# Weight sums of the down projection two pairs later, last token tiles built in place, key sums among the norms, and 66 low halves on GpSimd

## The chip, the cores and the metric

The kernel runs on one core of a Trainium2 chip. The metric is the device time of one execution in microseconds, and the kernel of before stands at the median of three runs. Besides TensorE, VectorE, ScalarE and GpSimd, the text speaks of SyncE (SP), which issues nearly all DMA transfers. The profile names the engines PE, DVE, ACT, POOL and SP.

## What is computed

One step of a two-layer encoder for two groups of rows: 1024 prompt positions and 8 × 16 sample positions, 1152 rows of width 1024, in the kernel nine token tiles of 128 rows (tile 8 holds the samples). Each layer is an attention and a GEGLU feed-forward with a causal convolution, both modulated by `c` and closed by a layer norm:

```python
def conv_ffn(h, prev, w_up, conv_w, conv_b, w_down):
    u = h @ w_up
    ...
    ue = jnp.concatenate([prev.astype(u.dtype), u], axis=1)
    y = conv_b
    for tap in range(CONV_W):
        y = y + conv_w[tap] * ue[:, tap:tap + T]
    a, g = jnp.split(y, 2, axis=-1)
    out = (jax.nn.gelu(g) * a) @ w_down
    return out, ue[:, T:]
...
        x = layer_norm(DEEPNORM_ALPHA * x + (1 + g_m) * mix, ln_g[l, 0], ln_b[l, 0])
        h = x * (1 + sc_f) + sh_f
        f, conv_rows = conv_ffn(h, None if prompt else state_conv[l], w_up[l], conv_w[l], conv_b[l], w_down[l])
        x = layer_norm(DEEPNORM_ALPHA * x + (1 + g_f) * f, ln_g[l, 1], ln_b[l, 1])
        if l == N_A_LAYERS - 1:
            ada_kv = (sc @ w_ada_kv + b_ada_kv)[:, None, :]
            sh_kv, sc_kv = jnp.split(ada_kv, 2, axis=-1)
            kv = ((x * (1 + sc_kv) + sh_kv) @ w_kv_b).reshape(B, T, 2, N_HEADS_B, HEAD_DIM)
```

D_MODEL is 1024, D_FF 2816 and there are two layers. After layer 0 one pair of keys and values is projected from its output (`w_kv_b`) and used by the attention of layer 1.

## The kernel before

**Stages.** Opening, attention, output projection, feed-forward (`ffn`, L1331 and around it) and down projection (`down`, L1419 on) of layer 0; then keys and values (`kv`, L836 on), attention, output projection, feed-forward and down projection of layer 1. One scheduler lays the instructions of each engine in a row ahead of time, and every engine and every DMA queue runs its row in that order.

**Split numbers.** Every fp32 operand of a large product is cast to a high half on ScalarE (L177), and the rest is made by a subtraction, the low half (L188), on VectorE or GpSimd as the caller's letters say ("v" or "p"). A product is three passes of matmuls: low by high, high by low, high by high.

**Seven products.** The large products of the feed-forward, the keys and the down projection halve their blocks by Strassen's scheme in Winograd's form: of two by two blocks, seven products instead of eight, from sums of blocks. There are three kinds of sums:

- Token sums (`tsums`, L1124 to 1152). For each of the nine token tiles the modulated transpose is reloaded from DRAM (`hD`, L1131), four sums are made (L1135 to 1138) and three of them split. For the feed-forward L1135 and L1136 run on GpSimd and a fourth sum is collected and cast once at the end (H); for the keys all four run on VectorE and the fourth is split tile by tile.
- Sums of up-weights (`products`, L1177 to 1180, on GpSimd) for each of the column pairs j = 2 to 21 of the feed-forward (pairs 0 and 1 are multiplied plainly) and for the keys' four. The matmuls of a pair are L1229, its evictions L1190 (VectorE) and L1197 (ScalarE).
- Sums for the down projection, made in spare time during the pairs. Two 128 × 512 blocks of a gated row pair give activation sums (`act_sums`, GpSimd, L1343 to 1346). Two rows of `w_down` give a weight sum (`weight_sums`, L1351 to 1359): two loads (L1354), three operations on GpSimd (L1355 to 1357) and two stores (L1358, L1359). There are eleven of each in a layer, and the list `wsum` says in which pair each weight sum is issued: `[2, 3, 4, 6, 8, ..., 20]`.

**Down projection.** Its products come in the order q = 1, 2, 5, 6, 3, 7, 4, each with eleven steps of twelve matmuls (L1476), fifteen where samples join. A step fetches one activation block and one weight block (`fetch`, L1491), splits both, and multiplies. The activations lie in a ring of seven slots (`acts`); their low halves are made by VectorE (L1471). The two sums q5 and u4, which become the left and the right half of the output of tiles 4 to 7, and c11 and p1, for tiles 0 to 3, stay in SBUF. `head` (L1533) adds the residual row to the two halves of a tile, into the residual's buffer (its home), and starts the norm; `tail` (L1566) finishes it: transposes on TensorE (L1042), the affine step on ScalarE (L1054), split of the transposed rows for the key and value products (L188, GpSimd in layer 0), stores of `hD` and `hmD`, and the norm's weight and bias (L1065 on GpSimd, L1066 on VectorE). Tile 8 is finished in product 3, tiles 0 to 3 in product 7, and tiles 4 to 7 after product 4. In layer 0 `zt` and `hf` are buffers of a tail: the copy of the transposed rows (one buffer or two), and the modulated ones (`hfr`, two buffers).

**Keys and values.** The value tiles of the first half are multiplied (L319) between the tails of tiles 4 to 7 and after them. The token sums of the keys go through a ring of four reload buffers (`raws`), which lie where q5 and u4 end; then come the key products and the value tiles of the second half.

Of the kernel before, what the change touches and what calls it, by code (L numbers as in the profile page):

```python
# [102 lines left out]
class Trunk:  # L103
# [732 lines left out]
    def kv(self, hv, vv):  # L836
# [11 lines left out]

        T1S = F[:, 6180:8484].rearrange("p (k t i) -> p k t i", k=4, i=64)
        p1s = [F[:, 8484:8804], F[:, 8804:9060]]  # L850
# [30 lines left out]
        order = (0, 1, 2, 3, 8, 4, 5, 6, 7)  # L881
        raws = Ring([F[:, o : o + 1024] for o in (2048, 3072, 4096, 5120)])
        for t in order[0:5]:
# [4 lines left out]
        last = self.wslots[2:4] + [(X2[:, o : o + 1024], X2[:, o + 1024 : o + 2048]) for o in (0, 2048)]  # L888
        hv, vv = Ring([F[:, o : o + 1024].bitcast(F32R) for o in (0, 1024)]), Ring([F[:, o : o + 512] for o in (11108, 11620)])
        for t in order[5:]:  # L890
# [29 lines left out]
        w = vload(1, last)  # L920
        hv = Ring(hl)
        self.ws = narrow
# [321 lines left out]
    def ffn(self, l, xsrc, xdst, affs):  # L1244
# [152 lines left out]
        self.pend = []  # L1397
        wsum = [2, 3] + list(range(4, NFF - 1, 2))
        for j in range(NPL):
# [19 lines left out]
    def down(self, l, xsrc, xdst, affs, act_sums):  # L1419
# [3 lines left out]
        def quad(x):  # L1423
            return [x[:, i * 512 : i * 512 + 512] for i in range(4)]

        X2 = self.x2p.tile([128, 4608], F32, name="x2f", tag="x2")
        q5, u4 = quad(F[:, 0:2048]), quad(F[:, 2048:4096])
        c11, p1 = quad(X2[:, 0:2048]), quad(X2[:, 2048:4096])
# [7 lines left out]
        homes = {8: fa, 0: fb, 1: self.w0[1], 2: fa, 3: fb, 4: X2[:, 0:1024], 5: X2[:, 2048:3072], 6: fa, 7: fb}  # L1436
        if l:
            homes[6], homes[7] = self.hf, self.gateS
        xs = {}
# [7 lines left out]
        late = Ring(raws)  # L1447
        diffs = Ring([F[:, o : o + 512] for o in range(2048, 6144, 512)])
        subs = self.subslots(ws[1:4])
# [13 lines left out]

        def act(src, sample=None):
            n = 512 if sample is None else 640
            hi, lo = (t[:, 0:n] for t in acts.next())
            raw = lo.bitcast(F32)
            nc.sync.dma_start(raw[:, 0:512], src)
            if sample is not None:
                nc.sync.dma_start(raw[:, 512:640], sample)  # L1470
            self.split(raw, hi, lo, "a", "v")  # L1471
            return hi, lo
# [18 lines left out]
        def fetch(q, m):  # L1491
# [15 lines left out]
            elif q == 6:  # L1507
                a, w = act(actS[m, 0][:, lo_half], sample(o)), weight(wT[m, 1][:, hi_half])
                w2 = weight(wdn[o][:, hi_half], late)
            elif q == 3:  # L1510
                a, w = act(actS[m, 1][:, lo_half]), weight(wdn[o][:, hi_half], late)
            elif q == 7:
                a, w = act(actS[m, 0][:, hi_half]), weight(wT[m, 0][:, hi_half])
            else:
                a, w = act(prompt(o, hi_half)), weight(wT[m, 1][:, lo_half])
            return a, w, w2 or w
# [17 lines left out]
        def head(t):  # L1534
# [5 lines left out]
            else:  # L1540
                parts = [q5[t - 4], u4[t - 4]]
            x = row = xs.pop(t)
            sm = self.sm.next() if l else None
            heads[t] = row, sm
# [58 lines left out]
        def tails(k):  # L1603
            def hook(m):
                if m in TAILS[k]:
                    t = TAILS[k][m]
                    tail(t)
                    rows(*{0: (3,), 1: (4, 5), 2: (6,), 3: (7,)}.get(t, ()))

            return hook  # L1610
# [29 lines left out]
        if not l:  # L1640
            self.take_w0(F32R)
            ev = [X2[:, o : o + 1024].bitcast(F32R) for o in (1024, 3072)], [X2[:, 4096:4608]]
            self.kvrun = self.kv(*ev)
# [292 lines left out]
```

## Time and profile before

| what | us |
| --- | --- |
| runs | 2814.4, 2820.66, 2827.81 |
| median | 2820.66 |
| profiled execution | 2813.54 |
| its span, from first to last instruction | 2811.8 |
| token sums of the feed-forward, layer 0 and layer 1 | about 485 to 541, 2020 to 2072 |
| pairs 2 to 21, layer 0 and layer 1 | 541 to 1050, 2072 to 2540 |
| down projection, layer 0 and layer 1 | 1050 to 1320, 2540 to 2812 |
| of it in layer 0, product 3 from, 7 from, 4 from | 1215, 1248, 1281 |
| keys and values, first half | 1320 to 1400 |

A row of the timeline has the start in the span, the duration, the engine, the line and operation, output and inputs by the program's names, the shape, and how many instructions in a row it stands for; in brackets stands how long the engine was idle before it, and which engine, buffer and line ended that. A group's row has the count, the busy time, the mean in ns and the idle time before. All positions are those of the profiled execution.

### The profile page before, as it was taken

The numbers are of one execution on the slowest core, as the hardware profiler recorded it, in microseconds if no ns is written. First come the engines' busy times: TensorE is split into PE (matmuls) and PEld (weight loads), VectorE is DVE, ScalarE is ACT, GpSimd is POOL, SyncE is SP. The second block draws the span as 40 slices with busy tenths as digits, with TensorE's granted clock in tenths as the row PEclk, the third lists the DMA queues.
The fourth block names the chain that finished last, engine by engine and source line by source line (L and its number), as shares of the span: only waits on it lengthen the run. The fifth ranks groups of instructions, "written<-read, shape, count | busy, mean of one in ns | idle before, by whom it ended". The sixth has DMA issues, their size and how long they took to land.

```text
span 2811.8 us, 47453 instructions
## 1 busy us (share of the span) xinstructions
PE 2657.6 (95%) x17134; PEld 2341.9 (83%) x17134; DVE 2031.0 (72%) x4010; ACT 1393.4 (50%) x2912; POOL 1031.4 (37%) x808
## 2 busy tenths in 40 slices
PE   7999889989999999998899999989989999999997
PEld 5887768889999997877798888867889999997775
DVE  4376767777777785679654677767888888885668
ACT  3475724443444344455636666663444444444554
POOL 2132523456555642112420122242465656542101
PEclk9999999999999999999999999999999999999998
DMA  8756444575565557675767467764453433347664
GB/s 296 222 163 190 141 131 158 186 275 198 190 206 201 186 169 245 199 246 194 279 205 266 114 162 197 215 193 142 156 189 112 143 134 130 132 145 249 199 211 151
DMA packets 252715, 528.59 MB, mean 188 GB/s; under 512 B 40032, under 2 KB 100400, under 8 KB 252480
## 3 DMA queue, kind: packets, MB, share of 16 engines
q1 hardware_dynamic: 252480, 525.56, 56.9%
q8 instruction: 135, 2.21, 0.3%
q14 instruction: 100, 0.82, 0.1%
HBM read 391.12 MB, written 143.77 MB: 190 GB/s over the span
## 4 chain that ended last, share of the span: by engine, by line
PE 69%; DVE 11%; DMA 10%; POOL 4%; issue 3%; ACT 3%; SPq 1%; DVEq 0%; POOLq 0%; ACTq 0%
PE PS L1229 26%; PE PS L1476 15%; PE PS L319 10%; PE PS L306 7%; PE PS L602 2%; PE PS L580 2%; DVE wl L188 2%; PE PS L234 2%; PE PS L551 1%; DMA w0f<-in_wdn_dram 1%; PE PS L293 1%; DMA actS<-F 1%; DMA ws<-in_adaw_dram 1%; DVE F L518 1%; PE PS L554 1%
## 5 line engine op out<-in xcount | busy, mean ns | idle before, releaser
L1229 PE MATMUL PS<-H,wh 128*128 128x256 f32 (+1 forms) x2624 | 408.6, 298 | 0.0
L1476 PE MATMUL PS<-wh,xa 128*128 128x512 f32 x1144 | 366.5, 400 | 17.5 <-ACT wh L177 6.4
L1229 PEld LDWEIGHTS PS<-H,wh 128*128 128x128 f32 x2624 | 373.1, 192 | 0.4 <-issue 0.4
L188 DVE TENSOR_TENSOR wl<-F,wh 128x512 fp32r<-128x512 f32 (+2 forms) x278 | 274.2, 996 | 31.6 <-ACT wh L177 29.1
L1190 DVE TENSOR_TENSOR F<-PS,F 128x320 f32<-128x320 f32 (+1 forms) x446 | 196.4, 450 | 130.3 <-PE PS L1229 129.2
L1476 PEld LDWEIGHTS PS<-wh,xa 128*128 128x128 f32 x1144 | 216.9, 190 | 74.4 <-ACT wh L177 12.4
L177 ACT CAST wh<-F 128x512 fp32r<-128x512 f32 (+2 forms) x278 | 163.7, 598 | 219.4 <-PE PS L1229 132.5
L1229 PE MATMUL PS<-H,wl 128*128 128x256 f32 (+1 forms) x1312 | 234.3, 301 | 22.2 <-ACT F L1197 15.8
L1476 PE MATMUL PS<-wl,xa 128*128 128x512 f32 x572 | 228.1, 400 | 0.4 <-DVE wl L188 0.4
L1229 PEld LDWEIGHTS PS<-H,wl 128*128 128x128 f32 x1312 | 196.7, 193 | 30.8 <-ACT F L1197 16.2
L1321 ACT ACTIVATE PS<-F 128x512 f32<-128x512 f32 x160 | 124.6, 779 | 187.6 <-DVE F L1323 107.2
L188 DVE TENSOR_TENSOR xa<-xa 128x640 fp32r<-128x640 f32 (+1 forms) x154 | 128.0, 836 | 122.2 <-ACT xa L177 121.1
L1229 PE MATMUL PS<-xa,wh 128*128 128x320 f32 (+1 forms) x1328 | 203.8, 296 | 0.0
L1331 POOL TENSOR_TENSOR F<-F 128x1152 f32<-128x1152 f32 x44 | 125.6, 2855 | 188.9 <-DVE F L1323 147.7
L177 ACT CAST xa<-xa 128x640 fp32r<-128x640 f32 (+1 forms) x154 | 104.0, 682 | 178.2 <-DMA xa<-actD 118.2
L1229 PEld LDWEIGHTS PS<-xa,wh 128*128 128x128 f32 x1328 | 186.3, 189 | 0.0
L177 ACT CAST wh<-ws 128x512 fp32r<-128x512 f32 (+1 forms) x153 | 104.3, 691 | 97.8 <-PE PS L1229 30.2
L1065 POOL TENSOR_TENSOR F<-F 128x1024 f32<-128x1024 f32 x24 | 58.6, 2443 | 227.8 <-PE PS L1042 95.1
L188 DVE TENSOR_TENSOR wl<-ws,wh 128x512 fp32r<-128x512 f32 (+1 forms) x135 | 135.7, 1011 | 8.4 <-ACT wh L177 7.9
L640 POOL TENSOR_TENSOR F<-F,x2r 64x512 f32<-64x512 f32 x62 | 79.4, 1281 | 168.2 <-DVE F L616 147.2
L319 PE MATMUL PS<-xa,H 128*128 128x512 f32 x504 | 133.3, 405 | 6.2 <-ACT xa L177 3.3
L306 PE MATMUL PS<-H,w0r 128*128 128x384 f32 (+1 forms) x720 | 138.3, 342 | 0.0
(349 smaller groups left out, 6384.2 us busy)
## 6 DMA issues: line engine op xcount, KB each, us to landing
ws<-in_adaw_dram SPq DMA_DIRECT2D x64, 512.0 KB
ws<-in_wup_dram SPq DMA_DIRECT2D x49, 512.0 KB
F<-in_adaw_dram SPq DMA_DIRECT2D x48, 512.0 KB
w0f<-in_wdn_dram SPq DMA_DIRECT2D x44, 512.0 KB
actS<-F SPq DMA_DIRECT2D x44, 512.0 KB
xa<-actS SPq DMA_DIRECT2D x88, 256.0 KB
F<-in_wup_dram SPq DMA_DIRECT2D x39, 512.0 KB
xa<-actD SPq DMA_DIRECT2D x66, 256.0 KB
```

Of the source, the lines that this page charges most:

```text
L177: nc.scalar.copy(out, in_)
L188: self.eng(el).tensor_sub(lo, src, hi.bitcast(F32))
L234: mm = nc.tensor.matmul(ps[32 * j : 32 * j + 32, hf * 256 : hf * 256 + 256], self.cT[:, k * 32 : k * 32 + 32], w[:, j * 256 : j * 256 + 25 ...
L306: mm = self.nc.tensor.matmul(out[:, 0:n], w[a][:, k * 128 : k * 128 + 128], H[:, p, k, s0 : s0 + n], start=i == 0, stop=i == 23)
L319: self.nc.tensor.matmul(out[:, 0:n], H[:, p, j * kn + k, t0 : t0 + 128], w[a][:, k * n : k * n + n], start=i == 0, stop=i == 23,)
L640: self.eng("v" if last else "p").tensor_mul(on[r, q], on[r, q], rb[r, :])
L1065: self.eng(er[0]).tensor_mul(xr, x, self.lng)
L1190: nc.vector.tensor_add(d, v(ps), a if len(a.shape) == 3 else v(a))
L1229: self.pairmm = nc.tensor.matmul(ps[:, 0:m], w[a][:, k * 128 : k * 128 + 128], x(p, k, n), start=start and c == 0, stop=c == 11, skip_grou ...
L1321: nc.scalar.activation(ps, u[:, 2 + o : 514 + o], AF.Identity, **aff)
L1331: nc.gpsimd.tensor_mul(yg, yg, ya)
L1476: self.downmm = nc.tensor.matmul(ps, a[p][:, i * 128 : i * 128 + 128], w[q], start=first and c == 0, stop=last and c == 2, skip_group_chec ...
```

## The change

Four edits:

1. `wsum` becomes `[4, 5, 6, 7, 8, 10, ..., 20]`: the first weight sum is issued in pair 4, and pairs 4 to 8 have one each.
2. In `down`, q5 and u4 are interleaved, so that the two halves of a tile 4 to 7 are 1024 neighbouring columns, and `head` writes the sum of these tiles there, in place, instead of into the residual's home. The homes of tiles 6 and 7 in layer 0 move, and both residuals are loaded after tail 3. The ring of weight differences (`diffs`) uses the gaps. The last four tails of layer 0 get one `hf` buffer, and `zt` lies at `fa`.
3. In `kv`, the buffers of the value tiles move, and the reload ring of the key sums has three slots, at columns 0 to 3071, which come free tile by tile; T1S moves by 36 columns.
4. `act` takes an engine for the low half, and products 3, 7 and 4 name GpSimd: 33 subtractions of 128 × 512 in each layer.

```diff
@@ kv
-        T1S = F[:, 6180:8484].rearrange("p (k t i) -> p k t i", k=4, i=64)
+        T1S = F[:, 6144:8448].rearrange("p (k t i) -> p k t i", k=4, i=64)
...
-        raws = Ring([F[:, o : o + 1024] for o in (2048, 3072, 4096, 5120)])
+        raws = Ring([F[:, o : o + 1024] for o in (0, 1024, 2048)])
...
-        hv, vv = Ring([F[:, o : o + 1024].bitcast(F32R) for o in (0, 1024)]), Ring([F[:, o : o + 512] for o in (11108, 11620)])
+        hv = Ring([F[:, o : o + 1024].bitcast(F32R) for o in (8448, 3072)])
...
-        hv = Ring(hl)
+        hv, vv = Ring(hl), Ring([F[:, o : o + 512] for o in (11108, 11620)])
@@ ffn
-        wsum = [2, 3] + list(range(4, NFF - 1, 2))
+        wsum = list(range(4, 9)) + list(range(10, NFF - 1, 2))
@@ down
-        q5, u4 = quad(F[:, 0:2048]), quad(F[:, 2048:4096])
+        q5, u4 = ([F[:, i * 1024 + o : i * 1024 + o + 512] for i in range(4)] for o in (0, 512))
...
-        if l:
-            homes[6], homes[7] = self.hf, self.gateS
+        homes[6], homes[7] = (self.hf, self.gateS) if l else (X2[:, 1024:2048], X2[:, 3072:4096])
...
-        diffs = Ring([F[:, o : o + 512] for o in range(2048, 6144, 512)])
+        diffs = Ring([F[:, o : o + 512] for o in (2560, 3584, 4096, 4608, 5120, 5632, 1536, 512)])
...
-        def act(src, sample=None):
+        def act(src, sample=None, el="v"):
...
-            self.split(raw, hi, lo, "a", "v")
+            self.split(raw, hi, lo, "a", el)
...
             elif q == 3:
-                a, w = act(actS[m, 1][:, lo_half]), weight(wdn[o][:, hi_half], late)
+                a, w = act(actS[m, 1][:, lo_half], el="p"), weight(wdn[o][:, hi_half], late)
             elif q == 7:
-                a, w = act(actS[m, 0][:, hi_half]), weight(wT[m, 0][:, hi_half])
+                a, w = act(actS[m, 0][:, hi_half], el="p"), weight(wT[m, 0][:, hi_half])
             else:
-                a, w = act(prompt(o, hi_half)), weight(wT[m, 1][:, lo_half])
+                a, w = act(prompt(o, hi_half), el="p"), weight(wT[m, 1][:, lo_half])
...
             x = row = xs.pop(t)
+            if 4 <= t < 8:
+                row = F[:, (t - 4) * 1024 : (t - 4) * 1024 + 1024]
...
-                    rows(*{0: (3,), 1: (4, 5), 2: (6,), 3: (7,)}.get(t, ()))
+                    rows(*{0: (3,), 1: (4, 5), 3: (6, 7)}.get(t, ()))
...
             self.take_w0(F32R)
-            ev = [X2[:, o : o + 1024].bitcast(F32R) for o in (1024, 3072)], [X2[:, 4096:4608]]
+            rings = Ring([fa]), Ring([self.hf])
+            ev = [F[:, 8448:9472].bitcast(F32R)], [F[:, 9472:9984]]
```

In GpSimd's row, the token sums of a feed-forward (L1135, L1136) read like this before from the sixth tile on; L1355 to L1357 are the first weight sum, L1331 the gating product of pair 1, and L1407 clears edges of the first Strassen pair.

```order
L1135 TENSOR_TENSOR F<-F 128x4x64
L1136 TENSOR_TENSOR F<-F 128x4x64
L1355 TENSOR_TENSOR w0f<-w0f 128x512
L1331 TENSOR_TENSOR F<-F 128x1152
L1356 TENSOR_TENSOR w0f<-w0f 128x512
L1135 TENSOR_TENSOR F<-F 128x4x64 x3
L1357 TENSOR_TENSOR w0f<-w0f 128x512
L1136 TENSOR_TENSOR F<-F 128x4x64 x3
L1407 MEMSET F 128x2
```

The same four tiles in the changed kernel:

```order
L1135 TENSOR_TENSOR F<-F 128x4x64
L1287 TENSOR_TENSOR F<-F 128x8x2
L1136 TENSOR_TENSOR F<-F 128x4x64
L1331 TENSOR_TENSOR F<-F 128x1152
L1135 TENSOR_TENSOR F<-F 128x4x64 x2
L1136 TENSOR_TENSOR F<-F 128x4x64
L1135 TENSOR_TENSOR F<-F 128x4x64
L1136 TENSOR_TENSOR F<-F 128x4x64 x2
L1407 MEMSET F 128x2
```

The three operations of the weight sum are gone from between the token sums; layer 1 reads the same way.

In GpSimd's row in the down projection of layer 0, before, the weight differences (L1503) are followed by nothing but tails, each an L1065 (norm weight) and a split (L188 into H), from tile 8 on:

```order
L1503 TENSOR_TENSOR F<-F 128x512 x7
L1065 TENSOR_TENSOR F<-F 128x1024
L188 TENSOR_TENSOR H<-F,H 128x8x128
L1065 TENSOR_TENSOR F<-F 128x1024
L188 TENSOR_TENSOR H<-F,H 128x8x128
L1065 TENSOR_TENSOR w0f<-w0f,F 128x1024
```

In the changed kernel, from the same place to tile 2, the activations' low halves are the rows with xa (lines here are those of the changed file, in which `fetch` stands one line higher):

```order
L188 TENSOR_TENSOR xa<-xa 128x512 x8
L1065 TENSOR_TENSOR F<-F 128x1024
L188 TENSOR_TENSOR xa<-xa 128x512
L188 TENSOR_TENSOR H<-F,H 128x8x128
L188 TENSOR_TENSOR xa<-xa 128x512 x16
L1065 TENSOR_TENSOR F<-F 128x1024
L188 TENSOR_TENSOR xa<-xa 128x512
L188 TENSOR_TENSOR H<-F,H 128x8x128
L188 TENSOR_TENSOR xa<-xa 128x512
L1065 TENSOR_TENSOR w0f<-w0f,F 128x1024
L188 TENSOR_TENSOR xa<-xa 128x512
L188 TENSOR_TENSOR H<-F,H 128x8x128
```

Twenty-five low halves stand ahead of tile 0's split and seven or eight more among the tails of tiles 0 to 2.

In VectorE's row where the tails of tiles 4 to 7 end and the key sums begin (L1066 is a tail's norm bias, L866 a value tile's low half, L1135 to L1138 a token tile's sums), before:

```order
L1066 TENSOR_TENSOR x2f<-x2f,F 128x1024
L866 TENSOR_TENSOR x2f<-PS,x2f 128x8x64 x2
L1066 TENSOR_TENSOR F<-F 128x1024
L866 TENSOR_TENSOR F<-PS,F 128x8x64
L1066 TENSOR_TENSOR F<-F 128x1024
L866 TENSOR_TENSOR F<-PS,F 128x8x64
L1135 TENSOR_TENSOR F<-F 128x4x64 x3
L1136 TENSOR_TENSOR F<-F 128x4x64 x3
```

and in the changed kernel, from the same tile's L1066, that of tile 5:

```order
L1066 TENSOR_TENSOR F<-F 128x1024
L1135 TENSOR_TENSOR F<-F 128x4x64
L866 TENSOR_TENSOR F<-PS,F 128x8x64
L1136 TENSOR_TENSOR F<-F 128x4x64
L1137 TENSOR_TENSOR F<-F 128x4x64
L1138 TENSOR_TENSOR F<-F 128x4x64
L188 TENSOR_TENSOR xa<-F,xa 128x4x64 x2
L188 TENSOR_TENSOR x2r<-F,x2r 128x4x64
L1066 TENSOR_TENSOR F<-F 128x1024
L866 TENSOR_TENSOR F<-PS,F 128x8x64
L1135 TENSOR_TENSOR F<-F 128x4x64
L1136 TENSOR_TENSOR F<-F 128x4x64
```

The first tile's sums stand before the norm bias of tile 6, and two more tiles' before that of tile 7.

## The prediction

> **What bounds the kernel now.** I read the page first, then the chain of the run, then what TensorE waited for.
>
> ```profile
> span 2811.8 us, 47453 instructions
> PE 2657.6 (95%) x17134; PEld 2341.9 (83%) x17134; DVE 2031.0 (72%) x4010; ACT 1393.4 (50%) x2912; POOL 1031.4 (37%) x808
> ...
> PE 69%; DVE 11%; DMA 10%; POOL 4%; issue 3%; ACT 3%; SPq 1%; DVEq 0%; POOLq 0%; ACTq 0%
> ```
>
> TensorE is busy 95% of the span and 69% of the final chain is its own, so about 150 us of 2811.8 are idle, and only idle time that ends because of an edited step can be won. The list of TensorE's waits (line waiting, what ended the wait: total, times, longest) names these:
>
> ```profile
> PE PS L1229 <- ACT F L1197: 15.8, 2, 8.9
> ...
> PE PS L1229 <- ACT xa L177: 9.1, 2, 8.9
> ...
> PE PS L319 <- DVE F L1634: 4.4, 1, 4.4
> ```
>
> The 15.8 us are one stall at the first pair after the token sums in each FFN; the 9.1 hold one of 8.9 before the key products; the 4.4 stand where the last token tiles begin. Next, busy time by stage (start:end length, then PE, PEld, DVE, ACT, POOL busy with counts, granted clock, DMA share, GB/s): the layer-1 token sums, steady pairs, the down product 7, the product 4, the tails beside the value tiles, and the key sums.
>
> ```profile
> 2030.00:2072.00 42.00, 33.08 (x195) 32.88 (x193) 37.43 (x70) 22.62 (x49) 22.83 (x27) 0.94 0.56 188
> 600.00:700.00 100.00, 98.95 (x768) 91.06 (x767) 73.53 (x110) 37.56 (x71) 60.67 (x47) 0.99 0.58 198
> 1240.00:1280.00 40.00, 40.00 (x177) 32.32 (x176) 36.85 (x87) 23.89 (x41) 6.57 (x2) 1.00 0.70 240
> 1280.00:1320.00 40.00, 37.06 (x164) 29.45 (x163) 36.60 (x43) 23.34 (x50) 17.23 (x7) 0.96 0.66 229
> 1340.00:1370.00 30.00, 30.00 (x149) 24.82 (x148) 11.08 (x18) 24.89 (x55) 20.30 (x12) 1.00 0.86 329
> 1370.00:1406.00 36.00, 26.08 (x140) 23.11 (x140) 33.14 (x92) 20.51 (x60) 12.05 (x5) 0.86 0.69 246
> ```
>
> In the token sums VectorE is busy 37.43 of 42 us and TensorE idles: VectorE sets the end there. In steady pairs TensorE is busy 98.95 of 100, so GpSimd's 60.67 cost nothing. In 1340 to 1370 TensorE is full and VectorE does only 11.08; right behind it VectorE has 33.14 of 36 and TensorE stops. That unevenness is what the key part of the change touches.
>
> **Part 1: weight sums start two pairs later.** The timeline of the layer-1 token sums (start, duration, engine, line, operands, and in brackets the idle time before it and who ended it):
>
> ```profile
> 2047.83 1.47 POOL L1355 TENSOR_TENSOR w0f<-w0f 128x512 f32<-128x512 f32 x1
> 2048.07 1.51 DVE L1137 TENSOR_TENSOR F<-F 128x256 f32<-128x256 f32 x1
> ...
> 2050.52 4.15 DVE L188 TENSOR_TENSOR xa<-F,xa 128x256 fp32r<-128x256 f32 x2 [0.48 <-ACT xa L177]
> ...
> 2052.91 1.48 POOL L1356 TENSOR_TENSOR w0f<-w0f 128x512 f32<-128x512 f32 x1
> ...
> 2055.58 0.32 SPq L1131 DMA_DIRECT2D F<-hD  x1
> ...
> 2059.70 0.75 PE L1229 MATMUL PS<-H,wl 128*128 128x320 f32 x4
> ...
> 2060.28 1.34 PE L1229 MATMUL PS<-H,wh 128*128 128x320 f32 x8
> 2060.32 1.30 POOL L1357 TENSOR_TENSOR w0f<-w0f 128x512 f32<-128x512 f32 x1
> ...
> 2061.58 2.31 POOL L1136 TENSOR_TENSOR F<-F 128x256 f32<-128x256 f32 x3
> ...
> 2071.97 1.44 PE L1229 MATMUL PS<-H,wl 128*128 128x320 f32 x4 [8.92 <-ACT F L1197]
> ...
> 2073.20 2.33 PE L1229 MATMUL PS<-H,wh 128*128 128x320 f32 x8
> ```
>
> L1355 to L1357 are the first weight sum. While L1355 runs (2047.83 to 2049.30), L1137 on VectorE takes 1.51 where the same shape takes about 0.42 (L1135 in the key sums' rows below): 1.1 lost. The two splits at L188 take 4.15 instead of 0.83 across L1331 and L1356; L1331 stays, L1356 owns about 1.4 of that. L1357 stands straight ahead of the last three L1136, whose tiles end the stage: 1.3. All three lie in front of the stall that ends at 2071.97, so 1.1 + 1.4 + 1.3 = 3.8 comes off it, and in layer 0, where the same three sums stand in the same places, the same. The weight sum's two loads and two stores leave SyncE's row there as well; the last reload of a tile was issued at 2055.58 between them and lands earlier, which I count as nothing, since VectorE is full. The stall of layer 0, and a later one:
>
> ```profile
> 540.64 1.43 PE L1229 MATMUL PS<-H,wl 128*128 128x320 f32 x4 [6.87 <-ACT F L1197]
> ...
> 596.57 2.90 DVE L188 TENSOR_TENSOR wl<-ws,wh 128x512 fp32r<-128x512 f32 x2
> ...
> 597.83 1.43 PE L1229 MATMUL PS<-H,wl 128*128 128x320 f32 x4 [4.25 <-DVE wl L188]
> ```
>
> After a stall the first four matmuls take 1.43 to 1.44 and the next eight 2.33; ahead of it the same shapes take 0.75 and 1.34 (at 2059.70 and 2060.28), so each stall costs some 2 us more behind it. With 8.92 − 3.8 = 5.1 left in layer 1 I count 0.5 of that as saved, per layer. Sum for both layers: 2 × (3.8 + 0.5) = 8.6, say −9. By the Trainium skill (TensorE: Matmul & The Clock Gate, section "HAM oscillation — how this bites in real kernels") the clock drops only behind gaps longer than about 3.4 us; the rows agree, and by that rule layer 0, left with 6.87 − 3.8 = 3.1, would keep full clock and the sum would be about 2 lower; I don't use this.
>
> The row at 597.83 is the second gain: the up-weight of pair 3 is split only from 596.57 to 599.47, with the loads, stores and sums of pairs 2 and 3's weight sums on the same queue and on GpSimd. Its 4.25 and some 2 of slow clock make 6.3; with those transfers two pairs later I take −5, bounds −6.3 (all of it theirs) to 0 (other background loads fill the gap).
>
> The moved sums now come in five pairs in a row (4 to 8) instead of every second one. Each is three GpSimd ops, 1.47 + 1.48 + 1.30 = 4.3 us in the rows above, with two 512 KB loads and two stores. A pair is 168 matmuls, so 100 us with 768 hold 4.6 pairs of 22 us, and GpSimd is busy 13 in each (60.67 in all): 4.3 more fits. The skews of layer 0 (L1673) share the queue. I take +1, bounds 0 to +4, a second late up-weight like the one above. Part 1: −9 − 5 + 1 = **−13**; bounds −18 (both stalls lose their slow clock too) to −3 (the two gains of layer 0's pairs lost, +4).
>
> **Part 2: 66 low halves to GpSimd.** The prices, from the groups by form (count, busy, mean ns, idle before); VectorE from 1210 to 1320,
>
> ```profile
> L188 DVE TENSOR_TENSOR xa<-xa 128x512 fp32r<-128x512 f32 x30 | 22.8, 767 | 6.3 <-ACT xa L177 6.2
> ```
>
> and the same view of GpSimd over the whole run:
>
> ```profile
> L1065 POOL TENSOR_TENSOR F<-F 128x1024 f32<-128x1024 f32 x24 | 58.6, 2443 | 227.8 <-PE PS L1042 95.1 <-DVE F L1032 51.9 <-ACT xa L177 26.1
> ...
> L188 POOL TENSOR_TENSOR H<-F,H 128x512 fp32r<-128x512 f32 x4 | 5.1, 1284 | 3.8 <-DVE C L518 3.1 <-ACT H L177 0.7
> ```
>
> Then the timeline in products 7 and 4:
>
> ```profile
> 1247.30 5.79 POOL L188 TENSOR_TENSOR H<-F,H 128x1024 fp32r<-128x1024 f32 x1 [7.38 <-ACT H L177]
> ...
> 1250.74 0.68 DVE L1617 TENSOR_TENSOR x2f<-PS,x2f 128x512 f32<-128x512 f32 x1
> ...
> 1251.45 2.18 DVE L188 TENSOR_TENSOR xa<-xa 128x512 fp32r<-128x512 f32 x1
> ...
> 1294.71 2.31 PE L1476 MATMUL PS<-H,xa 128*128 128x512 f32 x6 [2.19 <-DVE H L188]
> ...
> 1308.01 9.16 PE L1476 MATMUL PS<-H,xa 128*128 128x512 f32 x38 [0.74 <-DVE xa L188]
> ```
>
> One low half costs 0.77 on VectorE; nothing like it ran on GpSimd, but the nearest split of that size took 1.28. The three rows from 1247 show that the two engines exclude each other: a GpSimd split took 5.79, where L1065 with as many elements takes 2.44; it ended 2.35 after VectorE turned to an op with a PSUM source (L1617, 1250.74), and VectorE's next split waited, 2.18 instead of 0.77. So a move does not free 0.77; it adds 1.28 − 0.77 = 0.5 to the time in which one shuts out the other. The Trainium skill says the same (SBUF — State Buffer, section "Who interferes with whom"), and Perfetto Trace Analysis, section "Optimizing Scalar/DVE Operations", warns that offloading between these two might not help; by that the part would gain nothing, whose price from rows is the last rival below.
>
> Product 3's eleven fall where GpSimd is nearly idle: cost 0. Products 7 and 4 hold 22. Their windows have VectorE 36.85 + 36.60 = 73.5 of 80 and GpSimd 6.57 + 17.23 = 23.8. After: VectorE 73.5 − 22 × 0.77 = 56.5, GpSimd 23.8 + 22 × 1.28 = 52; the sum rises from 97.3 to 108.5, by 11.3. TensorE's step of 12 matmuls takes 2.9 us (38 in 9.16), and the activations' ring is seven deep, so up to 20 us of lag is covered in product 7. The risk is the end of product 4: eight of its low halves now stand between three tails' L1065 and splits in GpSimd's row, and TensorE needs the last one at 1308.01, where it already waited 0.74 on such a split. I take +3 in layer 0, bounds −3 (the stalls here go) to +11. In layer 1 GpSimd has only the norms' products, few and short of it: +1, bounds −2 to +5. Part 2: **+4**; bounds −5 to +16.
>
> **Part 3: key sums inside the norms.** The waits in the timeline, and the sums' price by the groups from 1340 to 1410:
>
> ```profile
> 1326.12 1.18 PE L319 MATMUL PS<-wh,H 128*128 128x512 f32 x2 [4.36 <-DVE F L1634]
> ...
> 1371.38 1.10 DVE L1135 TENSOR_TENSOR F<-F 128x256 f32<-128x256 f32 x3 [0.95 <-DMA hD<-F]
> ...
> 1395.46 1.43 PE L1229 MATMUL PS<-xa,w0r 128*128 128x320 f32 x4 [8.89 <-ACT xa L177]
> ```
>
> ```profile
> L188 DVE TENSOR_TENSOR xa<-F,xa 128x256 fp32r<-128x256 f32 x18 | 7.2, 413 | 0.0
> ...
> L1135 DVE TENSOR_TENSOR F<-F 128x256 f32<-128x256 f32 x9 | 3.5, 417 | 1.1 <-DMA hD<-F 1.0
> ```
>
> VectorE begins all nine token tiles' sums at 1371.38, after every norm. One tile has four sums and four splits or more, some 3.5 us (0.42 each), 31 us in all; TensorE stands 8.89 until 1395.46, and some 2 of slow clock follow as above. Afterwards VectorE has three tiles' sums, 10.5 us, done before the last norm, in the window where it does 11.08 of 30. That is more than the 8.89. Against it: the last tails of layer 0 share one buffer for their transposed rows where two stood, so a tail cannot begin its affine step until the split of the tail before it is done. GpSimd's two ops of a tail are 4.9 us by L1065's price, and the sums, 0.42 each alone, stop GpSimd and are stopped by it. Last, keys for tiles 6 and 7 still need these tiles' stores and reloads. I take **−7**, bounds −11 (stall and slow clock gone) to 0. The in-place rows remove no instruction; the 4.36 at 1326.12 waits for the last gate of product 4 and stays.
>
> **Sum.** −13 + 4 − 7 = −16 against the profiled execution's 2813.54 (span 2811.8 and 1.7 around it): 2797.5. The median shown, 2820.66, is 7.1 higher, so the forecast is **2805**.
>
> **The rivals.** *All cover holds*: no sum disturbs a later pair (−14), the low halves cost nothing, the key stall goes with its slow clock (−11), and product 4's waits go with the one behind it (2.19 + 0.74 + 4.36 = −7): −32, **2788**. For it speaks GpSimd's idleness, 37% busy in all; against it that VectorE keeps 37 of 42 us in the token sums. *Handed on*: the sums' wait is replaced by the next one in line, VectorE's own splits at the pairs' start and the hidden reload of tiles 6 and 7; 3 us are left, **2818**. For it speaks that L1331 and the conv taps in the same rows also delay VectorE. *GpSimd's row paces product 4*: the low halves wait their turn behind its eight tail ops (8 × 2.44 = 20), the 22 moves add 11 of exclusion, and the product runs at that pace: +31 − 13 from part 1 = +18, **2839**. It decides once the ring of seven is used up and a low half ends later than TensorE's step of 2.9 us asks; the 5.79 row speaks for it, GpSimd's 6.57 of 40 us in product 7 against it.
>
> **How the numbers follow.** Forecast 0.38 (own range 2797 to 2813, from the terms' nearer ends), all cover holds 0.25, handed on 0.20, GpSimd's row 0.17. The range runs from 2788 to 2831: it takes in the second and third cases and the upper ends of parts 1 and 2 together (2805 + 10 + 12 = 2827), and leaves out most of the fourth. A change under 0.5%, 14 us, cannot be told from none: below 2806.6 lie the second case and just over half of the forecast, 0.45; within, the rest of it and the third, 0.38; slower 0.17.
>
> **What would show it.** Right: no L1355 before pair 4, the stalls at the first pairs down from 6.87 and 8.92 to 3 to 5, no 4.25 in pair 3; L1135 on VectorE before the last L1066, and the key stall under 3. Wrong: TensorE waiting for GpSimd's L188 on activations in product 4, the tails 8 to 10 us apart, or late up-weights in pairs 4 to 8.

## The result, and the profile after

The changed kernel takes 2841.45 us (median of 4 runs, 2838.65 to 2845.95) against 2821.24 before (4 runs): a ratio of 1.0074, 95% interval 1.0052 to 1.0096, so 0.7% **slower**, where 2805 was forecast, in a range from 2788 to 2831. The profiled execution took 2841.3 us. The page has:

```profile
span 2839.5 us, 47474 instructions
PE 2667.6 (94%) x17134; PEld 2346.9 (83%) x17134; DVE 2047.9 (72%) x3944; ACT 1391.0 (49%) x2912; POOL 1130.4 (40%) x874
```

GpSimd is busy 99 us more (1130.4 against 1031.4), and VectorE, which gave 66 operations away, 17 us more, in 66 instructions fewer. At the 0.77 us that such an operation took before, the ones that VectorE kept take some 68 us longer (17 + 66 × 0.77, an estimate): what moved did not become free. The list of TensorE's waits:

```profile
PE PS L1475 <- ACT wh L177: 14.4, 10, 2.7
PE PS L1229 <- ACT F L1197: 12.7, 3, 7.3
PE PS L1475 <- DVE H L188: 11.2, 1, 11.2
...
PE PS L319 <- POOL H L188: 7.1, 2, 6.6
PE PS L1475 <- DVE F L1625: 6.9, 1, 6.9
...
PE PS L1475 <- POOL xa L188: 2.0, 2, 1.3
```

(L1475 here is L1476 before.) Against before, the waits behind the token sums fell from 15.8 to 12.7, the 6.4 on cast weights became 14.4, and three long new ones stand in product 4 (H), in the last tails of layer 0 (GpSimd's H) and at the end of product 7 in layer 1 (L1625). For the moved low halves themselves (GpSimd's xa) TensorE waits 2.0 us in the whole run. The stages, from the steady pairs on, with the token sums of layer 1 last:

```profile
600.00:700.00 100.00, 97.50 (x767) 89.79 (x766) 82.22 (x112) 37.21 (x72) 70.97 (x53) 1.00 0.70 245
1254.00:1288.00 34.00, 32.50 (x149) 26.10 (x148) 24.09 (x49) 21.48 (x42) 19.32 (x13) 1.00 0.54 179
1288.00:1328.00 40.00, 28.66 (x125) 22.60 (x124) 33.99 (x38) 17.57 (x36) 25.93 (x13) 0.87 0.61 211
1345.00:1375.00 30.00, 30.00 (x147) 24.76 (x146) 15.64 (x27) 23.48 (x48) 13.16 (x6) 1.00 0.64 231
1380.00:1416.00 36.00, 22.07 (x101) 18.98 (x100) 33.22 (x81) 24.53 (x68) 9.24 (x9) 0.80 0.88 304
2042.00:2084.00 42.00, 35.00 (x205) 34.67 (x203) 35.64 (x72) 22.62 (x48) 20.07 (x24) 0.96 0.46 136
```

Product 4 (1288 to 1328) has VectorE and GpSimd busy 33.99 + 25.93 = 60 of 40 us and TensorE only 28.66, at a granted clock of 0.87. The token sums are lighter than before on VectorE (35.64 against 37.43), and the key sums still have it busy 33.22 of 36, now with TensorE at 22.07 instead of 26.08. What happens in product 4 is in the timeline:

```profile
1296.87 0.62 ACT L177 CAST H<-H 128x512 fp32r<-128x512 f32 x1
...
1300.91 2.79 POOL L1065 TENSOR_TENSOR F<-F 128x1024 f32<-128x1024 f32 x1
1301.42 3.36 DVE L1066 TENSOR_TENSOR w0f<-w0f,F 128x1024 f32<-128x1024 f32 x1
1303.66 2.24 POOL L188 TENSOR_TENSOR xa<-xa 128x512 fp32r<-128x512 f32 x1
1304.70 1.75 DVE L1626 TENSOR_TENSOR F<-F 128x512 f32<-128x512 f32 x1
1305.86 2.79 POOL L188 TENSOR_TENSOR H<-F,H 128x1024 fp32r<-128x1024 f32 x1
...
1306.97 2.22 DVE L188 TENSOR_TENSOR H<-H 128x512 fp32r<-128x512 f32 x1
...
1309.25 3.35 PE L1475 MATMUL PS<-H,xa 128*128 128x512 f32 x7 [11.22 <-DVE H L188]
```

The two engines take turns without a gap: L1066 takes 3.36 where it takes 1.2 undisturbed (below: 1.23), L1626 then 1.75, and the low half on GpSimd 2.24 instead of the 1.28 that I had for it. The high half of the weight was there at 1297.5, its low half stands in VectorE's row behind all this until 1309.2, and TensorE stands 11.22 us. It is not GpSimd's low half that TensorE lacks, but VectorE's.

### The profile page after: what moved, and what is told of

It reads as the page before. It is cut to its first block, busy times and chain, and to the rows that moved or that the text cites. A ratio compares the mean times of both kernels' runs of the same rounds, so it can differ in the third digit from the quotient of the medians.

```text
span 2839.5 us, 47474 instructions
## 1 busy us (share of the span) xinstructions
PE 2667.6 (94%) x17134; PEld 2346.9 (83%) x17134; DVE 2047.9 (72%) x3944; ACT 1391.0 (49%) x2912; POOL 1130.4 (40%) x874
## 4 chain that ended last, share of the span: by engine, by line
PE 32%; DVE 11%; DMA 7%; POOL 3%; issue 3%; ACT 2%; SPq 0%; ACTq 0%; DVEq 0%; POOLq 0%
PE PS L1229 10%; PE PS L1475 7%; PE PS L319 6%; PE PS L306 4%; PE PS L602 1%; DVE wl L188 1%; PE PS L580 1%; DMA w0f<-in_wdn_dram 1%; DMA wl<-wT 1%; DMA xa<-actD 1%; DVE F L1323 1%; PE PS L551 1%; DVE F L518 1%; DVE F L1278 1%; DMA actS<-F 1%
## 5 line engine op out<-in xcount | busy, mean ns | idle before, releaser
L1475 PE MATMUL PS<-wh,xa 128*128 128x512 f32 x1144 | 372.5, 404 | 33.6 <-ACT wh L177 14.4
L188 DVE TENSOR_TENSOR wl<-F,wh 128x512 fp32r<-128x512 f32 (+2 forms) x278 | 278.4, 1012 | 24.7 <-ACT wh L177 22.6
L1475 PEld LDWEIGHTS PS<-wh,xa 128*128 128x128 f32 x1144 | 218.6, 192 | 92.7 <-ACT wh L177 18.7
L1229 PE MATMUL PS<-H,wl 128*128 128x320 f32 (+1 forms) x1312 | 233.4, 300 | 12.7 <-ACT F L1197 12.7
L1475 PE MATMUL PS<-wl,xa 128*128 128x512 f32 x572 | 230.2, 403 | 2.9 <-DVE wl L188 2.9
L1331 POOL TENSOR_TENSOR F<-F 128x1152 f32<-128x1152 f32 x44 | 124.8, 2836 | 183.2 <-DVE F L1323 136.9
L188 POOL TENSOR_TENSOR xa<-xa 128x512 fp32r<-128x512 f32 x66 | 100.2, 1525 | 191.2 <-ACT xa L177 190.1
L188 DVE TENSOR_TENSOR xa<-xa 128x640 fp32r<-128x640 f32 x88 | 84.9, 969 | 101.0 <-ACT xa L177 97.0
L188 DVE TENSOR_TENSOR wl<-ws,wh 128x512 fp32r<-128x512 f32 (+1 forms) x135 | 138.4, 1031 | 7.6 <-ACT wh L177 7.4
```

The lines of the kernel that those rows point to most:

```text
L188: self.eng(el).tensor_sub(lo, src, hi.bitcast(F32))
L1229: self.pairmm = nc.tensor.matmul(ps[:, 0:m], w[a][:, k * 128 : k * 128 + 128], x(p, k, n), start=start and c == 0, stop=c == 11, skip_grou ...
L1331: nc.gpsimd.tensor_mul(yg, yg, ya)
L1475: self.downmm = nc.tensor.matmul(ps, a[p][:, i * 128 : i * 128 + 128], w[q], start=first and c == 0, stop=last and c == 2, skip_group_chec ...
```

## Experiments

Each run is compared with the kernel before on the same chip, whose median goes from 2816.6 to 2821.2 us in the four sets of runs; so two runs are compared by their ratios. Theory G says that the low halves on GpSimd cost the time. The rivals are named where they come in. The table first; the edits and expectations follow.

| run | median, us | ratio to before (95%) |
| --- | --- | --- |
| later sums alone | 2803.25 | 0.9959 (0.9946 to 0.9972) |
| low halves alone | 2852.49 | 1.0126 (1.0109 to 1.0143) |
| places alone | 2828.55 | 1.0042 (1.0026 to 1.0057) |
| sums and places | 2810.93 | 0.9979 (0.9965 to 0.9993) |
| sums, product 3's halves | 2815.05 | 0.9981 (0.9968 to 0.9993) |
| sums, product 7's halves | 2816.2 | 1.0000 (0.9988 to 1.0012) |
| sums, product 4's halves | 2813.91 | 0.9995 (0.9980 to 1.0010) |
| added subtractions | 2872.64 | 1.0183 (1.0161 to 1.0206) |
| added clears | 2823.01 | 1.0017 (0.9998 to 1.0036) |
| late ring, places | 2820.84 | 1.0007 (0.9993 to 1.0020) |
| more hf, places | 2817.44 | 0.9997 (0.9981 to 1.0013) |
| four reloads, places | 2808.97 | 0.9978 (0.9965 to 0.9991) |

**The parts one by one.** Later sums alone:

```diff
-        wsum = [2, 3] + list(range(4, NFF - 1, 2))
+        wsum = list(range(4, 9)) + list(range(10, NFF - 1, 2))
```

> Only the weight sums begin later; everything else is as before. Theory G (the low halves on GpSimd cost the time, the later sums gain): about 15 us faster than before, 10 in layer 0's feed-forward and 4 in layer 1's, as the profile after has them between the output projection and the down projection; the stall at the first pair of layer 1 near 7 us instead of 8.9. Theory P (the new places of buffers cost the time, the rest moves nothing): the later sums alone are within 4 us of before.

Low halves alone, the `act(..., el="p")` lines of the change on the kernel before:

> Only the 66 low halves of products 3, 7 and 4 go to GpSimd; sums, places and key sums as before. Theory G: 20 to 30 us slower than before, with a stall of 8 us or more in product 4 of layer 0 that ends with VectorE's split of a weight, and one of 5 or more at the end of product 7 in layer 1. Theory P: within 6 us of before, no stall over 3 us in product 4.

Places alone, and sums and places together: the changed kernel without `el="p"`, with the old and with the new `wsum`:

> Only the places: in-place tiles 4 to 7, the moved rings, one hf buffer, key sums among the norms; the weight sums begin in pair 2 and all low halves stay on VectorE. Theory G: between 3 us faster and 6 us slower than before; the key stall falls from 8.9 to about 5, and a wait on GpSimd's split of 5 to 7 us appears in the value tiles. Theory P: 12 to 20 us slower, most of it in products 5 and 6, where the profile after has several waits for weights that it did not have before.

> The changed kernel with all activation low halves back on VectorE. Theory G: 8 to 16 us faster than before, so 28 to 36 faster than the changed kernel; no stall of over 4 us in product 4. Theory P: within 5 us of before, since the places eat what the sums gain.

The sums gain 0.41%, 12 us (13.6 between the medians), as theory G had it. The low halves alone cost 1.26%, 36 us, more than G's 20 to 30, and both stalls that G named are there: 8.60 us in product 4 of layer 0 and 7.94 at the end of product 7 in layer 1. On top of the other parts they cost 0.95% (1.0074 over 0.9979), 27 us. Theory P falls for the size of the loss, but the places are not free: 0.42% alone, some 12 us, twice G's limit of 6 and close to P's 12 to 20, and 0.2% on top of the sums (0.9979 over 0.9959), where the intervals overlap. Sums and places together are 6 us faster, below G's 8 to 16 and just outside P's 5. The three steps, −0.41, +0.20 and +0.95%, make up the 0.74% of the whole change.

The stretches between the first evictions behind the products (start of the first L1590, L1600, L1617, L1625 and L1634, or the same lines of each kernel, in one profiled execution each) say where:

| us, layer 0 / layer 1 | products 2, 5, 6 | 3 | 7 | 4 (layer 1: to its first subtraction) |
| --- | --- | --- | --- | --- |
| before | 124.5 / 121.1 | 33.3 / 36.8 | 30.4 / 37.6 | 33.6 / 12.3 |
| later sums alone | 122.7 / 122.5 | 34.6 / 35.3 | 30.4 / 37.7 | 33.6 / 12.1 |
| changed | 132.2 / 128.6 | 35.5 / 38.1 | 34.2 / 40.3 | 39.3 / 19.3 |
| low halves alone | 129.8 / 128.4 | 36.3 / 37.4 | 37.7 / 41.6 | 43.5 / 18.4 |
| sums and places | 124.1 / 120.7 | 31.7 / 35.6 | 31.4 / 37.7 | 36.3 / 12.3 |
| sums, product 3's halves | 127.3 / 126.7 | 33.8 / 37.1 | 30.9 / 37.7 | 34.7 / 12.1 |
| added subtractions | 125.2 / 123.9 | 42.6 / 40.2 | 36.0 / 46.5 | 40.6 / 18.2 |
| added clears | 119.2 / 122.0 | 34.7 / 34.5 | 32.0 / 39.4 | 41.3 / 14.4 |

The changed kernel loses 19.4 us in layer 0's row and 18.5 in layer 1's, in every product, not at the end of product 4 only.

**Which halves.** The later sums, and of the low halves one product's:

```diff
-                a, w = act(actS[m, 1][:, lo_half]), weight(wdn[o][:, hi_half], late)
+                a, w = act(actS[m, 1][:, lo_half], el="p"), weight(wdn[o][:, hi_half], late)
```

> The later weight sums, and of the low halves only product 3's eleven in each layer on GpSimd; places and key sums as before. Theory G, by place (GpSimd's row is nearly empty in product 3, so a half there shuts out nothing): within 3 us of the later sums alone, which were 13.6 us faster than before, so 10 to 17 us faster than before. Rival (each moved half costs, wherever it stands; 66 cost 36 us, so 22 cost 12): about 2 us faster than before.

> The later weight sums, and of the low halves only product 7's eleven in each layer on GpSimd. With product 3's costing 6 us and all 66 costing 36 alone, theory S gives product 7, whose stretch has VectorE busy 37 of 40 us, 8 to 14 us over the later sums alone: within 6 us of before. Rival (only product 4, where GpSimd's row holds three tails, costs): within 3 us of the later sums alone, 10 us or more faster than before.

> The later weight sums, and of the low halves only product 4's eleven in each layer on GpSimd. Theory S gives it the rest, 12 to 20 us over the later sums alone: 0 to 8 us slower than before, with a stall of over 4 us in product 4 of layer 0 on VectorE's split of a weight. Rival (products share alike): 6 us over the later sums alone, 7 faster than before.

Product 3's cost 0.22% over the later sums alone, 6 us, against the "within 3" of the emptier row; product 7's 0.41%, product 4's 0.36%, some 12 and 10 us. Each of the three is uncertain by some 5 us, product 3's most in proportion. Together they are 28 us, about as much as all of them in the changed kernel: 0.3 to 0.5 us for each of the 22 moved halves, wherever they stand. No product is free, against theory G for product 3 and against the rival for product 7. Product 7's share lies in theory S's 8 to 14; product 4's lies between its 12 to 20 and the rival's 6, and settles neither. The run with product 4's alone has the stall of the changed kernel at the same place:

```profile
1298.97 13.95 PE L1476 MATMUL PS<-H,xa 128*128 128x512 f32 x51 [12.56 <-DVE H L188]
```

**Shutting out or waiting in a row.** Added subtractions keep all of VectorE's work and give GpSimd as many subtractions, on top, whose result nothing uses:

```diff
             self.split(raw, hi, lo, "a", "v")
+            if extra:
+                nc.gpsimd.tensor_sub(X2[:, 4096:4608], hi.bitcast(F32), self.lng[:, 0:512])
```

> The kernel before with 33 more GpSimd subtractions of 128 x 512 in each layer, at the places of the changed kernel's low halves in products 3, 7 and 4, whose result nothing uses; VectorE keeps its low halves. Theory S (the two engines shut each other out, whoever needs the result): 20 us slower than before or more, with VectorE's low halves late in product 4 of layer 0. Theory W (TensorE waits for what stands behind GpSimd's tail operations in its row): within 6 us of before, since no low half moved.

Added clears put two GpSimd operations that only write at the same places, and even let the transfers wait for them:

```diff
             raw = lo.bitcast(F32)
+            for _ in range(2 * extra):
+                nc.gpsimd.memset(raw, 0.0)
```

> As the run with added subtractions, but the added GpSimd work is two clears of 128 x 512 per activation block of products 3, 7 and 4 (66 in each layer), of the slot that the block's transfer then fills; a clear reads nothing. GpSimd is busy about 1.0 us per block, near the 1.3 of a subtraction, at the same places of its row. Theory S (the shutting out needs both engines to read SBUF with two operands on VectorE): at most 15 us slower than before, against the 52 of the added subtractions. Theory W (the in-order row behind the tail operations is what costs; here even the transfers wait for it): 30 us slower than before or more.

The added subtractions, whose result nothing uses, cost 1.83%, 52 us for 66 operations; others wait for them only where three casts need a block that they still read, 4.1 us in all. Clears cost 0.17%, with an interval from none to 0.36%, 10 us. Groups from the end of layer 0's down projection: first one row of before (1210 to 1320) and one of the changed kernel, then the rows with subtractions, then those with clears (all 1200 to 1345). The rows with wl are low halves of weights, which VectorE makes in all four kernels:

```profile
L188 DVE TENSOR_TENSOR wl<-wl,wh 128x512 fp32r<-128x512 f32 x10 | 6.8, 679 | 1.6 <-ACT wh L177 1.6
...
L188 DVE TENSOR_TENSOR wl<-wl,wh 128x512 fp32r<-128x512 f32 x12 | 14.9, 1256 | 14.9 <-ACT wh L177 14.9
```

```profile
L1473 POOL TENSOR_TENSOR x2f<-xa,F 128x512 f32<-128x512 f32 x33 | 53.8, 1631 | 87.8 <-ACT xa L177 87.1
...
L188 DVE TENSOR_TENSOR xa<-xa 128x512 fp32r<-128x512 f32 x33 | 33.0, 1005 | 10.6 <-ACT xa L177 10.5
...
L188 DVE TENSOR_TENSOR wl<-wl,wh 128x512 fp32r<-128x512 f32 x14 | 16.2, 1154 | 1.4 <-ACT wh L177 1.4
```

```profile
L1469 POOL MEMSET xa<- 128x512 f32 x60 | 30.9, 526 | 35.2 <-PE PS L1478 33.8
...
L188 DVE TENSOR_TENSOR xa<-xa 128x512 fp32r<-128x512 f32 x32 | 27.7, 874 | 8.2 <-ACT xa L177 8.1
...
L188 DVE TENSOR_TENSOR wl<-wl,wh 128x512 fp32r<-128x512 f32 x12 | 8.2, 683 | 6.5 <-ACT wh L177 6.4
```

A subtraction holds GpSimd for 1631 ns beside VectorE, and VectorE's own low halves rise, those of activations from 767 to 1005, those of weights from 679 to 1154. Sixty clears are 30.9 us of GpSimd's time, but the low halves of weights stay at 683 and those of activations rise to 874 only. So it is the shutting out, theory S. The row alone (theory W) costs at most the 10 us of the interval, even with the transfers queued behind it. It is not shown to be free: in product 4 of layer 0 TensorE waits 2.96 and 1.66 us for late activations in the trace with clears, and the last column is 7.7 us longer than before, while products 2, 5 and 6 are 5.3 shorter. In layer 0 the clears also end ahead of the norm of tile 2, behind which the changed kernel still has four low halves. The Trainium skill has this too (SBUF — State Buffer, section "Who interferes with whom"): a VectorE instruction with two SBUF inputs contends with a GpSimd instruction that reads SBUF, not with one that only writes it. These two runs agree.

**The keys.** On sums and places, first the reload ring where it comes free after the last tail, then more hf buffers, then the four old slots; in the first and the third a buffer of the value tiles (`hv`) moves as well:

```diff
-        raws = Ring([F[:, o : o + 1024] for o in (0, 1024, 2048)])
+        raws = Ring([F[:, o : o + 1024] for o in (3072, 4096, 5120)])
...
-        hv = Ring([F[:, o : o + 1024].bitcast(F32R) for o in (8448, 3072)])
+        hv = Ring([F[:, o : o + 1024].bitcast(F32R) for o in (8448, 0)])
...
-            rings = Ring([fa]), Ring([self.hf])
+            rings = Ring([fa]), Ring([X2[:, 0:1024], X2[:, 1024:2048], self.hf, self.hf])
...
-        raws = Ring([F[:, o : o + 1024] for o in (0, 1024, 2048)])
+        raws = Ring([F[:, o : o + 1024] for o in (2048, 3072, 4096, 5120)])
...
-        hv = Ring([F[:, o : o + 1024].bitcast(F32R) for o in (8448, 3072)])
+        hv = Ring([F[:, o : o + 1024].bitcast(F32R) for o in (8448, 0)])
```

> The changed kernel with low halves on VectorE, and its reload ring at columns 3072 to 6143, which come free only after the last tail, so that the key sums follow the norms as before; in-place tiles and the single hf buffer stay. Theory H (the single hf buffer spaces the tails and costs what part 3 lost): as slow as the same kernel with early sums (6 us faster than before) or up to 6 us slower, the key stall back at 6 us or more, the tails still 8 to 10 us apart. Theory K (sums among the norms delay the tails and spread the wait): 5 to 10 us faster than the same kernel with early sums.

> The changed kernel with low halves on VectorE, and for the last four tails of layer 0 two more hf buffers in X2, free there since the rows are built in place; early key sums stay. Theory H: 4 to 8 us faster than the same kernel with one hf (6 us faster than before), so 10 to 14 us faster than before; tails 6 to 7.5 us apart. Theory K: within 3 us of it.

> The changed kernel with low halves on VectorE and the key sums' four reload buffers where they were, at columns 2048 to 6143, so that the sums follow the norms as before; in-place tiles and one hf stay. If the early sums gain what the places cost (theory K2): 5 to 10 us slower than the same kernel with early sums, so as fast as before to 4 us slower, with a key stall of 8 us or more. If the early sums gain nothing (theory N): within 3 us of that kernel, 3 to 9 us faster than before.

With three late slots the sums follow the norms and 0.28% is lost against early sums; I took this for the worth of the early sums until the third run: with the old four slots they follow the norms as well, and the time is that of the early sums, 0.9978 against 0.9979. So the early sums gain nothing (theory N), and the late ring of three was a handicap of its own. Theory H falls too: two more buffers gain nothing (0.9997), and the last tails come no closer, 10.2, 7.6 and 12.8 us from one L1066 to the next against 10.2, 8.1 and 10.5 with one buffer. One long wait has become several short ones. TensorE's stall with four reloads, and the same place with early sums (a row of each stall):

```profile
1391.03 1.44 PE L1229 MATMUL PS<-H,wl 128*128 128x320 f32 x4 [13.57 <-DVE wl L188]
```

```profile
1344.14 1.23 DVE L1066 TENSOR_TENSOR F<-F 128x1024 f32<-128x1024 f32 x1 [2.30 <-POOL F L1065]
...
1347.13 2.39 POOL L188 TENSOR_TENSOR H<-F,H 128x1024 fp32r<-128x1024 f32 x1 [3.02 <-ACT H L177]
1347.43 2.38 DVE L1135 TENSOR_TENSOR F<-F 128x256 f32<-128x256 f32 x1
...
1350.17 2.57 POOL L1065 TENSOR_TENSOR F<-F 128x1024 f32<-128x1024 f32 x1 [0.65 <-PE PS L1042]
1350.40 2.63 DVE L1136 TENSOR_TENSOR F<-F 128x256 f32<-128x256 f32 x1
...
1369.66 2.17 PE L1229 MATMUL PS<-H,w0r 128*128 128x256 f32 x12 [2.52 <-DVE w0r L188]
...
1374.96 3.57 PE L1229 MATMUL PS<-H,w0r 128*128 128x320 f32 x12 [3.12 <-DVE F L866]
1380.94 3.52 PE L1229 MATMUL PS<-xa,w0r 128*128 128x320 f32 x12 [2.42 <-DVE w0r L188]
1388.13 1.23 PE L1229 MATMUL PS<-xa,w0r 128*128 128x256 f32 x4 [3.67 <-ACT xa L177]
```

L1135 and L1136 take 2.38 and 2.63 instead of 0.42 when they meet GpSimd's share of a tail (L188, L1065): in the window where VectorE had been idle, GpSimd was not. The four stalls are 2.52, 3.12, 2.42 and 3.67, 11.7 us in all, against the one of 13.57. The sums do end earlier, the last L1138 at 83 us behind the first eviction of product 4 (L1635) against 94 with four reloads, but the last matmul of the key products starts 172.4 us behind that eviction against 174.2, and before it was 170.2.

## Why the prediction was wrong, by its steps

**Part 1 held.** −13 was forecast, −12 to −13.6 measured, but its inside was sized wrong, so that the total agrees is in part luck. In the run with later sums alone the two first-pair stalls are

```profile
539.32 1.43 PE L1229 MATMUL PS<-H,wl 128*128 128x320 f32 x4 [5.16 <-ACT F L1197]
```

```profile
2061.61 1.44 PE L1229 MATMUL PS<-H,wl 128*128 128x320 f32 x4 [7.18 <-ACT F L1197]
```

5.16 and 7.18 instead of 6.87 and 8.92: 1.7 less each, not 3.8. In the 42 us up to the end of layer 1's stall VectorE is busy 34.76 us instead of 37.43, but it waits 1.68 us instead of 0.48 for ScalarE's cast before the last splits, which takes part of the gain back. The late weight of pair 3 is gone with its slow clock, 6.4 us where the upper bound had 6.3 (by the evictions at L1197 that trace is 1.6 ahead at 568 of before and 8.0 at 629), and layer 1 gained 2.6 by its last pairs, those 1.7 among them. Heavier pairs 4 to 8 cost nothing that shows.

**Part 2 failed.** The step reads: "So a move does not free 0.77; it adds 1.28 − 0.77 = 0.5 to the time in which one shuts out the other." The price was right: 66 × 0.5 = 33, and the runs gave 27 on top of the other parts and 36 alone. What failed was the next step, which let the seven slots of the ring, GpSimd's idle time and product 3 cover it: +3 in layer 0, +1 in layer 1, 0 in product 3, so +4 in all. The runs showed no cover in any of them. The ring covers a late activation, but what came late was VectorE's own next operation, the low halves of weights, which stand in the row that was shut out; a deep ring of their own (eleven slots for the eleven steps of product 4 in layer 0) did not help them. And VectorE was already busy 36.85 of 40 in product 7. That window, where TensorE waited for nothing, hid that VectorE was within 8% of being the bound. In layer 1, which I priced at +1 because GpSimd had little to do there (before, 7.6 of the 87 us of products 3 to 4), the loss is as large as in layer 0, 18.5 against 19.4: it does not take a row full of tail operations on GpSimd; the moved halves and VectorE's own two-input operations are enough. Perfetto Trace Analysis of the Trainium skill, section "Optimizing Scalar/DVE Operations", which warns that such a move might not help, was right here: the runs show a loss of 27 to 36 us.

**Part 3 failed by its sign.** −7 was forecast; the early sums are worth nothing within some 5 us (the two intervals), and the whole part, places with early sums, costs 6 to 12. "Afterwards VectorE has three tiles' sums, 10.5 us, done before the last norm" came true, but in a window in which they take turns with GpSimd's tails. The single hf, my reason for the upper end, is not what cost it.

**The rivals.** The last, *GpSimd's row paces product 4*, at 2839, came within 3 us of the time, with a chance of 0.17. Its mechanism is half right: the two engines' exclusion is what costs, but TensorE waits for VectorE, product 4 has a third of the loss, and GpSimd's order behind tails does little: the clears put its worth at 10 us at most, and in the changed kernel TensorE waits 2.0 us in all for GpSimd's low halves. That the time agrees is in part chance, since it put all of the loss into layer 0. The range ended at 2831 because I took part 2's upper end, +16, as a bound, although its own price times its own count, 0.5 × 66, gives 33.

Open: 7.7 and 7.5 us of the loss stand in products 2, 5 and 6, ahead of most moved halves. The run with product 3's halves has 4.6 and 4.2 there over the later sums alone (122.7 and 122.5), but kernels without moved halves differ as much from trace to trace (119.2 to 126.5 in layer 0, 118.9 to 125.9 in layer 1), and the added subtractions show little of it; so neither that these halves cause it nor what carries it back is shown. What the places cost can be located, not explained: the five kernels with the new places and all low halves on VectorE take 36.2 to 36.3 us in the last column of layer 0 instead of 33.6, with a wait of 3.8 to 4.0 us for VectorE's low half of a weight where it was 2.2, and the key products end 2 to 7 us later behind it.

## What to carry to other kernels

Before moving an elementwise operation with two SBUF inputs from VectorE to GpSimd, look at how full VectorE is in that stage, price the move at GpSimd's duration less VectorE's, and take nothing off for GpSimd's idle time: 0.5 us each was the price here, 0.3 to 0.5 the loss, even where TensorE waited for neither engine. The plain sum of both engines' busy time is no test, as it also counts work that does not collide: in the steady pairs before it is 134 of 100 us, and TensorE is full. A ring ahead of the consumer covers a late result, but not the other work in the row of the engine that is shut out. And split the change: the one-line move of the weight sums alone is the best kernel here, 0.41% faster than before (interval 0.28% to 0.54%) and 1.1% faster than the whole change (0.9959 over 1.0074).

## What the runs showed of the hardware

GpSimd operations that only write left VectorE's pace nearly alone, and were left alone by it: the 132 clears took 515 to 539 ns each and cost 5 us, the 66 subtractions 1277 to 2616 ns and 52 us, for 2 × 0.526 = 1.05 us of GpSimd per block against 1.63.

Slow matmuls behind a gap do not go by the gap's length alone. After 4.51 us in the changed kernel's layer 0 the first four took 1.44 and the next eight 2.33; after 4.36 with sums and places the first four took 0.85, and only the next eight were slow, 2.16 where eight took 1.34 ahead of the gap:

```profile
542.76 1.44 PE L1229 MATMUL PS<-H,wl 128*128 128x320 f32 x4 [4.51 <-ACT F L1197]
543.99 2.33 PE L1229 MATMUL PS<-H,wh 128*128 128x320 f32 x8
```

```profile
536.92 0.85 PE L1229 MATMUL PS<-H,wl 128*128 128x320 f32 x4 [4.36 <-ACT F L1197]
537.61 2.16 PE L1229 MATMUL PS<-H,wh 128*128 128x320 f32 x8
```

And among the key stalls with early sums, shown above, twelve matmuls of 128 × 320 took 3.57 and 3.52 after gaps of 3.12 and 2.42 us. Without a gap twelve of that shape took 1.92 in the kernel before:

```profile
1407.86 1.92 PE L1229 MATMUL PS<-xa,w0r 128*128 128x320 f32 x12
```

The prediction's "only behind gaps longer than about 3.4 us" does not fit these two stalls. Four gaps follow each other within 20 us there, and whether one alone would do it no run shows.
